# One encoder layer on one core: last short score tile of a head pair in a gate bank, one activation product behind the next difference, one operand's cast moved in its table

## The chip, the core and the metric

The kernel runs on one core of a Trainium2 chip. The core has a matmul engine (TensorE, in the profile PE, with its weight loads as PEld), a vector engine (VectorE, DVE), a scalar engine (ScalarE, ACT), a general engine (GpSimd, POOL) and a queue engine that issues most transfers (SyncE, SP). Matmul results go to PSUM banks and are read from there by DVE and ACT. The metric is the device time of one execution in microseconds (us); lower is better. Differences of less than about 0.2% of it, 4 us, can't be told from none.

## The reference, cut to what matters

One layer for two requests: a prompt of 1024 tokens and a sample of 32 tokens with caches, 1056 tokens in all, width 1024, feed-forward width 2816.

```python
h = _rms_norm(x, g_pre_mix)
z = h @ w_in
qa, ka, va, qb, fb, ib, ob, ga, gb = jnp.split(z, SPLIT_POINTS, axis=-1)
# A: sliding-window attention, 16 heads of width 64, 2 kv heads, sinks, relative bias
s = jnp.einsum('bnqkgd,bnskd->bnkgqs', q, k).astype(jnp.float32) * (A_HEAD_DIM ** -0.5)
...
p = jnp.exp(s - m)
denom = jnp.sum(p, axis=-1, keepdims=True) + jnp.exp(sink - m)
ya = jnp.einsum('bnkgqs,bnskd->bnqkgd', (p / denom).astype(v.dtype), v)
# B: gated linear recurrence, 8 heads
yb, s_fin = _hgrn2(...)
mix = jax.nn.sigmoid(ga) * (ya @ w_br_a) + jax.nn.sigmoid(gb) * (yb @ w_br_b)
x = x + _rms_norm(mix @ w_out, g_post_mix)
hf = _rms_norm(x, g_pre_ffn)
a, u = jnp.split(hf @ w_up, 2, axis=-1)
...                                   # ac: causal convolution of a over 3 tokens
ffn = (jax.nn.gelu(ac, approximate=True) * u) @ w_down
x = x + _rms_norm(ffn, g_post_ffn)
x = x + (pe @ w_ple) * jax.nn.sigmoid(x @ w_ple_gate)
```

## The kernel before

Everything is computed with activations transposed, features on the 128 partitions and tokens along the row. Each fp32 operand is split in two parts, a high one (a cast on ACT) and a low one (the difference, on DVE), and a product is three matmuls: high by high, high by low, low by high (`product`, L203 to L205). The engines run side by side, each through its own list of instructions in order; a scheduler makes those lists from the program, and where the code says `behind(engines)`, what is issued inside must stand behind the last instruction already issued on those engines. An instruction waits on semaphores for its inputs and for the last reader of a buffer that it is to write.

**Scores and gates.** Tokens lie in three groups of 384, 384 and 288. The heads are worked in eight pairs i. Around the scores of a pair run blocks of `w_in` columns (the next pair's q, and gates), each into a bank of the tag "mm". A pair has nine score tiles j: 0 to 7 for the prompt and 8 for the sample (64 rows, "short"). For a tile, `scores` makes the scores in a bank "s", softmax runs over them on DVE and ACT (probabilities `sc`, or `sc8` for tile 8; L509 to L514), `turn` transposes the probabilities into a bank (L535, for tile 8 L529) and splits them in a high and a low part (`split`: L226 on ACT, L227 on DVE), and `values` multiplies them by the values (L554, L555) into a bank "o" and adds the parts up (L561 on ACT, L562 and L563 on DVE). For tile 8 the result of `values` lies in the same bank as the turned probabilities, in its last quarter (`o8`), so that bank is held until L563 has read it. A q block that is done is split by `q_out`: L416 (ACT), L417 (DVE), L419 (ACT), L420 (DVE); a gate block is read by L295 (ACT). PSUM has here three banks "mm", two "tr", two "s" and one "o" (L238 to L248), each tag used in rotation. `turn` takes an "mm" bank for tiles 4 and 7, and a "tr" bank else. In four of the pairs (`H_AT`) DVE also adds up sums of h for a later stage (`h_sums`, L574 and on).

**The end of the second stage.** Before the up units, `ple_product` runs over four groups with a table `beside` of small steps between its matmuls: `at(m, f, ..., on=engines)` puts f at step m, behind what the named engines have been given. Among them are the last operands of the up units' products, made in place from four quarters b11, b21 (the page z[2]) and b12, b22 (z[3]): `minus` subtracts (L1899), L1919 adds, and `op_part(1, j, src)` casts a quarter to its high part (L1685, ACT) and takes the low part (L1686, DVE). The results of `ple_product` are copied out on ACT (L1732) and stored with a transfer that POOL issues (L1734).

**The up units.** For each of the 22 blocks of 128 features, `up_unit` makes both halves of the up product, for all tokens, by a scheme of seven products (0 to 6) over quarters of the operands, in three double banks X, Y, Z ("st"). The weights come split: L1756 (ACT), L1757 (DVE), with sums that POOL makes (L1770). After the products, `after(i)` takes what is ready: L2020 copies X to s1c (ACT), L2022 takes a difference U2, L2024 writes part of `ab`, L2027 writes nU3 = Y - s1c, L2029 and L2031 write the second half `us`, L2038 and others the rest. s1c, U2, nU3 and t12 lie in one tile `Sp`, the page that z[3] held. For product 5 PE writes Y again, so it must wait for L2027; for product 6 it writes Z again and waits for L2029. Unit 0 is run in two passes, over half of the tokens each; in the others a product is 24 matmuls of 264 columns (two halves of the tokens, four row blocks, the three lines L2009 to L2011).

`ff_tail(f, ab, u)`, a generator, is the rest of a unit: convolution (L1945, L1949, L1953), Gelu (L1954, ACT), the activation product (L1955 for 1024 columns, L1956 for the 32 of the sample) and its store act_d (L1957, on SP). Its first piece runs at the end of its unit (`done`), the rest behind product 1 of the next unit (`tail_rest`).

Of the kernel before, what the change touches and what calls it, by code (L numbers as in the profile page):

```python
# [21 lines left out]
NF = 22  # L22
# [37 lines left out]
def layer_kernel(  # L60
# [17 lines left out]
    def nm(s):  # L78
        n_names[0] += 1
        return f"{s}_{n_names[0]}"  # L80
# [5 lines left out]
    V, S, G, E = nc.vector, nc.scalar, nc.gpsimd, nc.tensor  # L86

    def behind(*engines):

        st = ExitStack()  # L90
        for e in engines:
            ins = next(i for i in reversed(nc.cur_bb.bb.instructions) if i.engine == e.engine)
            st.enter_context(tc.issue_after(ins))
        return st
# [128 lines left out]
    def split(hi, lo, src, scale=None):  # L223

        if scale is None:
            S.copy(hi, src)  # L226
            V.tensor_tensor(lo, src, hi.bitcast(F32), op=ALU.subtract)  # L227
        else:
            S.mul(hi, src, scale)
            V.scalar_tensor_tensor(lo, src, scale, hi.bitcast(F32), op0=ALU.mult, op1=ALU.subtract)  # L230

    def bank(pool, tag, bufs):
        return pool.tile([P, 512], F32, tag=tag, name=nm(tag), bufs=bufs)
# [4 lines left out]
    def mm_bank():  # L238
        return bank(pp, "mm", 3)

    def tr_bank():
        return bank(pp, "tr", 2)
# [35 lines left out]
    def unit(out):  # L278

        cell = []  # L280

        def get_w():
            if not cell:
                cell.append(next_w())
            return cell[0]
        return [(get_w, g, out) for g in range(3)]
# [4 lines left out]
    def gate_out(dst):  # L291
        def out(g, b):
            o, n = GR[g]
            t = gtile()
            S.activation(t[:, :n], b[:, :n], AF.Tanh, scale=0.5)  # L295
            dma(dst[:, o:o + n], t[:, :n])
        return out
# [17 lines left out]
    with right("ap") as ap:  # L315
# [148 lines left out]
        def span(j):  # L464

            if j == 8:
                return 32, 1024, 160, 0, ((8, 0, P), (9, P, 32))
            if j == 0:
                return P, 0, P, P, ((0, P, P),)
            return P, (j - 1) * P, 256, 0, ((j - 1, 0, P), (j, P, P))  # L470
# [48 lines left out]
        def turn(i, j):  # L519
            m_, k0, nk, b0, tl = span(j)  # L520
            sc = probs.get((i, j))
            ph = aq.tile([P, 2, 2 * P], F32R, tag="ph", name=nm("ph"), bufs=4)
            pl = aq.tile([P, 2, 2 * P], F32R, tag="pl", name=nm("pl"), bufs=4)
            t = mm_bank() if j in (4, 7) else tr_bank()
            n = 2 * len(tl) * m_
            ph, pl = (x[:].rearrange("p a b -> p (a b)")[:, :n] for x in (ph, pl))
            if j == 8:
                for a in range(2):
                    E.transpose(t[:, a * P:(a + 1) * P], sc8[:, a * P:(a + 1) * P], ident[:])  # L529
                split(*(x.rearrange("p (a b) -> p a b", b=64) for x in (ph, pl)),  # L530
                      t[:, 0:2 * P].rearrange("p (a b) -> p a b", b=P)[:, :, :64])
            else:
                for a, (_, kc, _) in enumerate(tl):
                    for h in range(2):
                        E.transpose(t[:, (2 * a + h) * P:(2 * a + h + 1) * P], sc[:, h, kc:kc + P],  # L535
                                    ident[:])
                split(ph, pl, t[:, :n])
            probs[i, j] = (ph, pl)
            if j == 8:
                o8[i] = t[:, 2 * P:3 * P]  # L540
# [387 lines left out]
        for i in range(8):  # L928
# [7 lines left out]
            if i == 0:  # L936
                rows_at = [lambda n=n: v_rows[n]() for n in range(9)] + [cache_parts]
                rows_at += [lambda n=n: k_rows[n]() for n in range(2)]
                for m, f in zip((0, 0, 1, *range(2, 20)), rows_at):
                    on = (E, S, V) if f is cache_parts else (E,)  # L940
# [17 lines left out]
            for j in range(9):  # L958
                at = lo_ + (hi_ - lo_) * j // 9
# [119 lines left out]
    with right("bp") as bp:  # L1079
# [311 lines left out]
        def at(m, f, *a):  # L1391
            small.setdefault(m, []).append(lambda: f(*a))
# [50 lines left out]
        u, v = (unit(gate_out(dst)) for dst, _ in GATES[14:])  # L1443
# [27 lines left out]
    with right("mp") as mp:  # L1471
# [33 lines left out]
        for b_, (c, g) in enumerate(order):  # L1505
            if c == len(ws):
                ws.append(next_w())
            o, n = G4[g]
# [311 lines left out]
    def prepare(n):  # L1820

        while n_parts[0] < min(n + 1, 7 * NF):
            u, i = divmod(n_parts[0], 7)
            if i == 0:
                if u not in raw_w:
                    unit_raw(u)
                s1 = wp.tile([P, 4, P], F32, tag="wb", name=nm("sa"), bufs=8)[:]
                gens[u] = unit_parts(u, s1, part_tile, lambda i, t: ready_w.append(t))
            next(gens[u])
            if i == 3 and u + 1 < NF:  # L1830
                unit_raw(u + 1)
            n_parts[0] += 1
# [40 lines left out]
    t = tr_bank()  # L1873
# [27 lines left out]
    def q_rows(g, i):  # L1901
        return z[g][:, 4 * i:4 * i + 4, :].bitcast(F32)

    b11, b21, b12, b22 = q_rows(2, 0), q_rows(2, 1), q_rows(3, 0), q_rows(3, 1)
# [13 lines left out]
    at(21, minus, b12, b22)  # L1918
    at(21, lambda: V.tensor_tensor(b22, b22, b11, op=ALU.add))  # L1919
    at(23, op_part, 1, 1, b22, on=(S,))  # L1920
    at(23, minus, b21, b22)
    at(25, op_part, 1, 3, b12, on=(S,))
    for g in range(4):
        ple_product(g, beside)
    assert not beside
# [9 lines left out]
    def ff_tail(f, ab, u):  # L1935

        w0, w1, w2 = (cvec[:, j * NF + f:j * NF + f + 1] for j in range(3))
        bc = cvec[:, 3 * NF + f:3 * NF + f + 1]
        n = T + 2
        a = fp.tile([P, T + 2], F32, tag="a", name=nm("a"), bufs=2)  # L1940
        V.tensor_copy(tails[:, 0, :, f], ab[:, 1024:1026])
        V.tensor_copy(tails[:, 1, :, f], ab[:, 1058:1060])
        with behind(V):
            V.tensor_copy(ab[:, 1026:1028], cach[:].rearrange("p (j f) -> p j f", j=2)[:, :, f])
        S.activation(a[:], ab[:, 0:n], AF.Identity, scale=w0, bias=bc)  # L1945
        if f < 3:
            V.tensor_tensor(u, u, rbT[:], op=ALU.mult)
            yield
        V.scalar_tensor_tensor(a[:], ab[:, 1:1 + n], w1, a[:], op0=ALU.mult, op1=ALU.add)  # L1949
        if f > 2:  # L1950
            V.tensor_tensor(u, u, rbT[:], op=ALU.mult)
            yield
        V.scalar_tensor_tensor(a[:], ab[:, 2:2 + n], w2, a[:], op0=ALU.mult, op1=ALU.add)  # L1953
        S.activation(a[:], a[:], AF.Gelu_apprx_tanh)  # L1954
        V.tensor_tensor(u[:, 0:1024], a[:, 0:1024], u[:, 0:1024], op=ALU.mult)  # L1955
        V.tensor_tensor(u[:, 1024:T], a[:, 1026:1058], u[:, 1024:T], op=ALU.mult)  # L1956
        dma(act_d[f][:], u)  # L1957
        yield

    tail_of = []  # L1960

    def tail_rest():
        for t in tail_of:
            next(t)
        tail_of.clear()

    def last_ops(n):

# [23 lines left out]
    def up_unit(u):  # L1992
# [7 lines left out]
        def mults(i, t, first, ps):  # L2000
            n = 7 * u + i
            if i not in w:
                w[i] = ready_w[n]
            for p in ps:
                for k in range(4):
                    wh, wl = w[i][:, 0, k, :], w[i][:, 1, k, :]
                    xh, xl = ops[p][i][:, 0, k, :], ops[p][i][:, 1, k, :]
                    o = t[:, p, 0:H]
                    E.matmul(o, wh, xh, start=first and k == 0, stop=False, skip_group_check=True)  # L2009
                    E.matmul(o, wh, xl, start=False, stop=False, skip_group_check=True)  # L2010
                    E.matmul(o, wl, xh, start=False, stop=k == 3, skip_group_check=True)  # L2011
# [43 lines left out]
        for ps, steps in (((0,), first_), ((1,), early)) if u == 0 else (((0, 1), order),):  # L2055
            for n, (i, t, first, then) in enumerate(steps):
                if u:
                    prepare(7 * u + n + AHEAD)
                elif ps == (1,):
                    with behind(S, V):  # L2060
                        prepare(n + AHEAD + 2)
                mults(i, t, first, ps)
                if ps == (1,) and n == 1:
                    with behind(E):
                        x1_t.append(pair_norm(1, 1.0 / D, late=True))
                if ps == (1,) and n == 4:
                    with behind(E):
                        x1_t[0]()
                for a in then:
                    with behind(*((V,) if ps == (0,) and a == 2 else ())):  # L2070
                        after(a, ps)
                if n == 1:
                    with behind(V):
                        tail_rest()
                if u == 0 and ps == (0,):
                    last_ops(n)
        done()
# [2 lines left out]
    for u in range(NF):  # L2080
        if u == 1:
            Up = page(lq, 2, [P, 2, T], "Up")
        if u == NF - 1:
            limit[0] = len(plan)
            load_raw()
            load_raw()
        up_unit(u)
    tail_rest()


    chunk_at = (("l4", "r3"), ("l6", "r5"), ("l7", "r6"), ("r0", "r7"))
# [103 lines left out]
    for s, dst in ((0, o_pconv), (1, o_sconv)):  # L2195
        b = tr_bank()
        E.transpose(b[:44, 0:P], tails[:, s].rearrange("p j f -> p (j f)"), ident[:])
        t = ep.tile([44, P], F32, tag="t", name=nm("tl"), bufs=6)
# [97 lines left out]
```

## Time and profile before

| | |
|---|---|
| median of three runs | 1984.14 us (1982.86 to 1984.45) |
| the profiled execution | 1983.89 us |
| its span | 1982.1 us |
| granted clock of TensorE | 0.999 |
| instructions | 37207 |
| turns of the score tiles (L535), in the span | 65.3 to 341.0 us |
| up units, first L2020 to last L1956 | 1167.5 to 1631.6 us |

The profile is of one execution. Times in it count from the start of its span, and the time of the execution is the span and 1.8 us around it. A row of the timeline gives start, duration, engine, line, operation, what is written and what is read with their shapes; in brackets stands how long the engine had been idle before it, and which instruction of another engine released it by the profile's reckoning. That name is the one that came last by the semaphores, and can be a neighbour of the true one. Rows of the view of waits have engine, line, whom it waited for, and then us in all, times and the longest.

### The profile page before, as it was taken

How to read it: one execution, taken by the hardware profiler on the slowest of the kernel's cores; microseconds unless marked ns; L12 is line 12 of the kernel's file. 1: busy time of each engine (PE TensorE's matmuls, PEld its weight loads, DVE VectorE, ACT ScalarE, POOL GpSimd, SP SyncE). 2: the span in 40 equal slices, each digit the busy share in tenths (PEclk: the TensorE clock that was granted, in tenths of full speed). 3: DMA queues.
4: the chain of work that ended last, by engine and by line, in shares of the span. 5: the costliest groups of instructions: out<-in, count | busy, mean ns of one | idle time of the engine just before them, and what ended most of it. 6: DMA issues, size and time to landing. Idle time of an engine off the chain costs nothing.

```text
span 1982.1 us, 37207 instructions
## 1 busy us (share of the span) xinstructions
PE 1962.2 (99%) x14239; PEld 1947.3 (98%) x14239; DVE 1387.5 (70%) x3059; ACT 1003.5 (51%) x2188; POOL 258.2 (13%) x391
## 2 busy tenths in 40 slices
PE   8999999999999999999999999999999999999998
PEld 8999999999999999999999999999999999999998
DVE  6777776888888888653555878877777784655552
ACT  7667767666656666451225663333333344444332
POOL 2111110000000000012001133333343300000000
PEclk9999999999999999999999999999999999999999
DMA  8533432311122121486558672222222255665542
GB/s 268 156 90 104 129 111 59 129 47 58 56 79 58 55 59 54 127 254 214 181 164 277 207 235 87 76 87 65 89 74 77 86 164 187 213 196 171 163 135 78
DMA packets 255256, 253.57 MB, mean 128 GB/s; under 512 B 14133, under 2 KB 221992, under 8 KB 255077
## 3 DMA queue, kind: packets, MB, share of 16 engines
q1 hardware_dynamic: 244917, 218.43, 35.3%
q0 software_dynamic: 10080, 32.73, 5.4%
q8 instruction: 112, 1.84, 0.4%
q14 instruction: 67, 0.55, 0.1%
q10 hardware_dynamic: 80, 0.03, 0.0%
HBM read 177.89 MB, written 65.32 MB: 123 GB/s over the span
## 4 chain that ended last, share of the span: by engine, by line
PE 90%; DVE 4%; ACT 2%; issue 2%; DMA 1%; POOL 0%; SPq 0%; DVEq 0%; ACTq 0%; POOLq 0%
PE mm L203 13%; PE mm L205 13%; PE mm L204 13%; PE st L2011 7%; PE st L2010 7%; PE st L2009 7%; PE G L1114 2%; PE Y L1111 2%; PE G L1113 2%; PE Y L1114 2%; PE G L1111 2%; PE Y L1113 2%; PE Z L1111 1%; PE Z L1113 1%; PE Z L1114 1%
## 5 line engine op out<-in xcount | busy, mean ns | idle before, releaser
L2009 PE MATMUL st<-op,wt 128*128 128x264 f32 x1232 | 348.7, 283 | 3.2 <-DVE Sp L2027 2.1
L2011 PE MATMUL st<-op,wt 128*128 128x264 f32 x1232 | 349.8, 284 | 0.0
L2010 PE MATMUL st<-op,wt 128*128 128x264 f32 x1232 | 347.7, 282 | 0.0
L2009 PEld LDWEIGHTS st<-op,wt 128*128 128x128 f32 x1232 | 231.2, 188 | 4.6 <-DVE Sp L2027 2.5
L2010 PEld LDWEIGHTS st<-op,wt 128*128 128x128 f32 x1232 | 231.4, 188 | 0.0
L2011 PEld LDWEIGHTS st<-op,wt 128*128 128x128 f32 x1232 | 230.9, 187 | 0.0
L182 ACT CAST wh<-wr 128x1024 fp32r<-128x1024 f32 x125 | 131.2, 1050 | 188.4 <-PE mm L204 146.2
L184 DVE TENSOR_TENSOR wl<-wr,wh 128x1024 fp32r<-128x1024 f32 x114 | 139.5, 1224 | 111.7 <-ACT wh L182 99.7
L1756 ACT CAST wt<-wu 128x512 fp32r<-128x512 f32 x126 | 77.8, 619 | 185.8 <-POOL ab L1995 82.3
L203 PE MATMUL mm<-ac,wh 128*128 128x352 f32 x528 | 170.6, 323 | 0.0
L205 PE MATMUL mm<-ac,wl 128*128 128x352 f32 x528 | 169.7, 321 | 0.0
L204 PE MATMUL mm<-ac,wh 128*128 128x352 f32 x528 | 169.4, 321 | 0.0
L203 PE MATMUL mm<-La,wh 128*128 128x384 f32 (+1 forms) x480 | 158.2, 330 | 0.0
L204 PE MATMUL mm<-Lb,wh 128*128 128x384 f32 (+1 forms) x480 | 155.3, 324 | 0.6 <-DVE Lb L773 0.6
L205 PE MATMUL mm<-La,wl 128*128 128x384 f32 (+1 forms) x480 | 154.8, 323 | 0.2 <-DVE wl L748 0.2
L203 PE MATMUL mm<-Ra,wh 128*128 128x264 f32 x512 | 145.4, 284 | 0.0
L204 PE MATMUL mm<-Rb,wh 128*128 128x264 f32 x512 | 145.0, 283 | 0.0
L205 PE MATMUL mm<-Ra,wl 128*128 128x264 f32 x512 | 145.0, 283 | 0.0
L1757 DVE TENSOR_TENSOR wt<-wu,wt 128x512 fp32r<-128x512 f32 x126 | 100.9, 803 | 47.1 <-ACT wt L1756 47.0
L205 PEld LDWEIGHTS mm<-ac,wl 128*128 128x128 f32 x528 | 99.4, 188 | 0.0
L204 PEld LDWEIGHTS mm<-ac,wh 128*128 128x128 f32 x528 | 99.3, 188 | 0.0
L203 PEld LDWEIGHTS mm<-ac,wh 128*128 128x128 f32 x528 | 99.0, 188 | 0.0
(553 smaller groups left out, 5746.4 us busy)
## 6 DMA issues: line engine op xcount, KB each, us to landing
wr<-in_w_down_dram SPq DMA_DIRECT2D x66, 512.0 KB
wu<-in_w_up_dram SPq DMA_DIRECT2D x42, 512.0 KB
wu<-in_w_in_dram SPq DMA_DIRECT2D x36, 512.0 KB
ac<-act_d SPq DMA_DIRECT2D x66, 176.0 KB
act_d<-Up SPq DMA_DIRECT2D x21, 528.0 KB
wr<-in_w_in_dram SPq DMA_DIRECT2D x21, 512.0 KB
wr<-in_w_out_dram SPq DMA_DIRECT2D x16, 512.0 KB
wl<-wr POOLq DMA_DIRECT2D x11, 512.0 KB, 4.9
```

Of the source, the lines that this page charges most:

```text
L182: S.copy(hi[:], raw[:])
L184: V.tensor_tensor(lo[:], raw[:], hi[:].bitcast(F32), op=ALU.subtract)
L203: E.matmul(ps, wh, a, start=first and n == 0, stop=False)
L204: E.matmul(ps, wh, b, start=False, stop=False)
L205: E.matmul(ps, wl, a, start=False, stop=last and n == len(ks) - 1)
L1111: E.matmul(o, wh, x[0][k], start=first and k == 0, stop=False, skip_group_check=True)
L1113: E.matmul(o, wh, x[1][k], start=False, stop=False, skip_group_check=True)
L1114: E.matmul(o, wl, x[0][k], start=False, stop=k == 3, skip_group_check=True)
L1757: V.tensor_tensor(t[:, 1], src, t[:, 0].bitcast(F32), op=ALU.subtract)
L2009: E.matmul(o, wh, xh, start=first and k == 0, stop=False, skip_group_check=True)
L2010: E.matmul(o, wh, xl, start=False, stop=False, skip_group_check=True)
L2011: E.matmul(o, wl, xh, start=False, stop=k == 3, skip_group_check=True)
```

## The change

There are three parts. `turn` takes an "mm" bank for tile 8 too, so that its values result lies in that bank as well. In `ff_tail` the unit 0 tail gets one more stop between Gelu and the activation product: `tail_rest(u)` no longer clears the list in unit 1, and behind product 3 of unit 1, after its `after(3)`, it is called again and runs the product and its store. (For f of 1 and more there is no such stop.) In the table `beside`, the step that casts operand 3 of the second half is put at 23, and the subtraction b21 - b22 at 25; they change places.

```diff
-            t = mm_bank() if j in (4, 7) else tr_bank()
+            t = mm_bank() if j in (4, 7, 8) else tr_bank()
...
     at(23, op_part, 1, 1, b22, on=(S,))
-    at(23, minus, b21, b22)
-    at(25, op_part, 1, 3, b12, on=(S,))
+    at(23, op_part, 1, 3, b12, on=(S,))
+    at(25, minus, b21, b22)
...
         S.activation(a[:], a[:], AF.Gelu_apprx_tanh)
+        if f < 1:
+            yield
         V.tensor_tensor(u[:, 0:1024], a[:, 0:1024], u[:, 0:1024], op=ALU.mult)
         V.tensor_tensor(u[:, 1024:T], a[:, 1026:1058], u[:, 1024:T], op=ALU.mult)
         dma(act_d[f][:], u)
...
-    def tail_rest():
+    def tail_rest(u):
         for t in tail_of:
             next(t)
-        tail_of.clear()
+        if u != 1:
+            tail_of.clear()
...
                 if n == 1:
                     with behind(V):
-                        tail_rest()
+                        tail_rest(u)
+                if u == 1 and n == 3:
+                    with behind(V):
+                        tail_rest(0)
...
-    tail_rest()
+    tail_rest(NF)
```

Behind `ff_tail` the lines of the changed kernel stand two or three higher: L1955 is L1957 there, L1956 is L1958, L2020 is L2023, L2022 is L2025, L2024 is L2027, L2027 is L2030, L2029 is L2032.

On PE, at tile 8 of a pair, the rows were these (the second s and the mm are the next score tile and the next block; what an instruction waits for stands in brackets, as engines):

```order
L529 MATMUL tr_2068<-ident,sc_811 128x128 [waits DVE_49,PE_49,Activation_49]
L529 MATMUL tr_2068<-ident,sc_811 128x128 [waits Pool_49]
L498 MATMUL s_2075<-K_0_186,qa_1627 128x256 [waits PE_49]
L499 MATMUL s_2075<-K_0_188,qa_1627 128x256
L498 MATMUL s_2075<-K_0_186,qb_1628 128x256
L499 MATMUL s_2075<-K_0_188,qb_1628 128x256
L203 MATMUL mm_2090<-La_177,wh_1576 128x384 [waits Activation_49]
L204 MATMUL mm_2090<-Lb_181,wh_1576 128x384
```

and they are now:

```order
L529 MATMUL mm_2068<-ident,sc_811 128x128 [waits DVE_49,Activation_49]
L529 MATMUL mm_2068<-ident,sc_811 128x128 [waits Pool_49]
L498 MATMUL s_2075<-K_0_186,qa_1627 128x256 [waits PE_49]
L499 MATMUL s_2075<-K_0_188,qa_1627 128x256
L498 MATMUL s_2075<-K_0_186,qb_1628 128x256
L499 MATMUL s_2075<-K_0_188,qb_1628 128x256
L203 MATMUL mm_2090<-La_177,wh_1576 128x384 [waits DVE_49]
L204 MATMUL mm_2090<-Lb_181,wh_1576 128x384
```

No row changes its place; tile 8 has another bank, and the block behind it waits for DVE and no longer for ACT.

On DVE, in up unit 1 (us is unit 0's second half, wt the split weights, Sp holds nU3), the rows were these:

```order
L2024 TENSOR_TENSOR ab_15178<-st_15175,rbT 128x2x264
L1757 TENSOR_TENSOR wt_15352<-wu_15130,wt_15352 128x512
L1955 TENSOR_TENSOR us_14887<-a_15168,us_14887 128x1024
L1956 TENSOR_TENSOR us_14887<-a_15168,us_14887 128x32
L2027 TENSOR_TENSOR Sp_14888<-st_15176,Sp_14888 128x528
L1757 TENSOR_TENSOR wt_15395<-wu_15132,wt_15395 128x512
L2029 TENSOR_TENSOR Up_15174<-Sp_14888,st_15177 128x2x264
```

and they are now:

```order
L2027 TENSOR_TENSOR ab_15178<-st_15175,rbT 128x2x264
L1757 TENSOR_TENSOR wt_15352<-wu_15130,wt_15352 128x512
L2030 TENSOR_TENSOR Sp_14888<-st_15176,Sp_14888 128x528
L1957 TENSOR_TENSOR us_14887<-a_15168,us_14887 128x1024
L1958 TENSOR_TENSOR us_14887<-a_15168,us_14887 128x32
L1757 TENSOR_TENSOR wt_15395<-wu_15132,wt_15395 128x512
L2032 TENSOR_TENSOR Up_15174<-Sp_14888,st_15177 128x2x264
```

The difference stands ahead of the two parts of the product; what comes behind is as it was.

On ACT, at the end of `ple_product` (op_14835 is operand 3 before, op_14819 in the changed kernel, op_14816 operand 1 in both; Sp is s1c of unit 0), the rows were these:

```order
L1732 COPY ple_14779<-st_14801 128x528
L1732 COPY ple_14820<-st_14821 128x528
L1685 CAST op_14835<-z_13343 128x1056
L1732 COPY ple_14820<-st_14838 128x528
L1732 COPY ple_14853<-st_14854 128x528
L1685 CAST op_14816<-z_13343 128x1056
L1732 COPY ple_14853<-st_14868 128x528
L2020 COPY Sp_14888<-st_14889 128x264
```

and they are now:

```order
L1732 COPY ple_14779<-st_14801 128x528
L1732 COPY ple_14822<-st_14823 128x528
L1732 COPY ple_14822<-st_14838 128x528
L1732 COPY ple_14853<-st_14854 128x528
L1685 CAST op_14816<-z_13343 128x1056
L1685 CAST op_14819<-z_13343 128x1056
L1732 COPY ple_14853<-st_14868 128x528
L2023 COPY Sp_14888<-st_14889 128x264
```

The cast of operand 3 stood two copies ahead of operand 1's, and now stands right behind it. On DVE the low parts (L1686) of the two follow in the same order: operand 3's, which stood ahead of the last L1899, is now the last of all.

## The prediction

> **What bounds the kernel now.** I read the busy line of the page first, then the chain of waits, then the list of what each engine waited for, and then the timeline around each place that the change touches.
>
> ```profile
> PE 1962.2 (99%) x14239; PEld 1947.3 (98%) x14239; DVE 1387.5 (70%) x3059; ACT 1003.5 (51%) x2188; POOL 258.2 (13%) x391
> PE 90%; DVE 4%; ACT 2%; issue 2%; DMA 1%; POOL 0%; SPq 0%; DVEq 0%; ACTq 0%; POOLq 0%
> PE tr L535 <- ACT qb L419: 3.4, 5, 0.8
> PE st L2009 <- DVE Sp L2027: 2.1, 2, 1.9
> PE st L2009 <- ACT Sp L2020: 0.9, 1, 0.9
> ```
>
> TensorE (PE) is busy for 1962.2 of 1982.1 us, and neither its matmuls nor their sizes change. So the change can only be worth what it adds to or takes from PE's stops. The three last rows (engine, line, whom it waited for: us in all, times, longest) are the three stops near the three edits: 6.4 us together, and a ceiling for what is to be gained, but for the small correction that follows. A matmul starts about 0.12 us after the one before it though each runs 0.28 (1206.50 and 1206.62 below), so a stop costs about 0.16 more than its idle figure.
>
> **First edit: the bank of the last short score tile.** The stop stands at the turn of a new head pair:
>
> ```profile
> 151.23 0.50 ACT L514 ACTIVATE sc<-sc,st 128x256 f32<-128x256 f32 x1
> 151.57 0.55 DVE L417 SCALAR_TENSOR_TENSOR qa<-mm,qa 64x384 fp32r<-64x384 f32 x1
> 151.84 0.29 PE L205 MATMUL mm<-La,wl 128*128 128x288 f32 x1
> 152.16 0.48 ACT L419 ACTIVATE qb<-mm 64x384 fp32r<-64x384 f32 x1
> 152.35 0.19 DVE L563 TENSOR_TENSOR ya<-tr,u 64x32 f32<-64x32 f32 x1
> 152.69 0.63 PE L535 MATMUL tr<-ident,sc 128*128 128x128 f32 x4 [0.56 <-ACT qb L419]
> 153.23 0.56 DVE L420 SCALAR_TENSOR_TENSOR qb<-mm,qb 64x384 fp32r<-64x384 f32 x1
> ```
>
> The view names L419, but a transpose of probabilities has no use for qb, and L419 ends at 152.64, just beside another candidate: the last read of the tr bank that tile 8 and its values sit in, L563, which ends at 152.54, 0.15 before PE starts again. There are two tr banks; the turn at 152.69 is the second one after tile 8, so it needs tile 8's bank. L563 is late because it stands on VectorE (DVE) behind L417. With tile 8 in an mm bank this turn needs only a tr bank that was read long before and its probabilities, ready at 151.73 (L514); PE comes at about 151.97. The stop goes. Over five boundaries that is 3.4 + 5 x 0.16 = 4.2 us, the most this edit can bring.
>
> What it adds is waits on the mm banks, three in rotation. The block of matmuls after tile 8 now takes the bank of turn 7, and tile 8 takes the one that the gate block left:
>
> ```profile
> 138.77 0.47 ACT L295 ACTIVATE gt<-mm 128x384 f32<-128x384 f32 x1
> 142.23 0.69 DVE L227 TENSOR_TENSOR pl<-mm,ph 128x512 fp32r<-128x512 f32 x1
> 143.46 0.38 PE L529 MATMUL tr<-ident,sc 128*128 128x128 f32 x2
> 144.16 0.34 PE L203 MATMUL mm<-La,wh 128*128 128x384 f32 x1
> ```
>
> Tile 8 at 143.46 needs L295, over at 139.24: 4.2 us early. The block at 144.16 needs turn 7's low part, over at 142.92: 1.24 us early. Both cost nothing, but if that low part were 1.24 us later, PE would stop there, with the four score matmuls and the whole block behind it.
>
> Where does the removed time go next? PE comes earlier to turns whose banks DVE or ScalarE (ACT) empty at a pace of their own:
>
> ```profile
> 161.94 0.41 ACT L295 ACTIVATE gt<-mm 128x288 f32<-128x288 f32 x1
> 163.04 0.60 PE L535 MATMUL mm<-ident,sc 128*128 128x128 f32 x4
> 223.79 0.63 PE L535 MATMUL tr<-ident,sc 128*128 128x128 f32 x4 [0.84 <-ACT qb L419]
> 224.86 0.56 DVE L574 TENSOR_TENSOR hs<-La,Lb 128x384 f32<-128x384 f32 x1
> 225.45 0.42 DVE L227 TENSOR_TENSOR pl<-tr,ph 128x256 fp32r<-128x256 f32 x1
> 226.34 0.60 PE L535 MATMUL tr<-ident,sc 128*128 128x128 f32 x4
> 176.00:211.00 35.00, 34.29 (x244) 34.02 (x242) 23.14 (x77) 25.99 (x69) 3.93 (x14) 1.00 0.45 124
> 211.00:247.00 36.00, 35.16 (x248) 34.82 (x247) 27.35 (x86) 25.66 (x69) 6.83 (x19) 1.00 0.37 102
> ```
>
> At the third boundary (223.79, stop 0.84 + 0.16 = 1.0) DVE works without a pause through two sums of h (L574), so L227 still ends at 225.87, and the turn at 226.34 has only 0.47 to spare: about 0.32 of the 1.0 stays won, after the 0.15 of a restart. The fourth boundary reads the same, 35.6 us later. At the first (0.72) the turn at 163.04 has 0.69 to spare on L295 (over at 162.35): about 0.6 stays. In the second and fifth there are no sums of h (the windows, in order us, PE, PEld, DVE: 23.14 us of DVE against 27.35), so they keep all, 4.2 - 0.72 - 1.0 - 0.73 = 1.75. Together 0.6 + 0.32 + 0.32 + 1.75 = **-3.0 us**, between -1.8 (if the second and fifth keep only a third, 0.6) and -4.2. The last head's turns are put in a new order on PE; the stops in it are a few tenths each, and I take **-0.2**, between +0.3 and -0.4, as an estimate.
>
> **Second edit: the first unit's activation product behind the difference.** In up unit 1:
>
> ```profile
> 1203.09 1.22 DVE L1955 TENSOR_TENSOR us<-a,us 128x1024 f32<-128x1024 f32 x1
> 1203.29 2.14 POOL L1770 TENSOR_TENSOR wu<-wu 128x512 f32<-128x512 f32 x1 [1.14 <-DVE wt L1757]
> 1204.23 1.26 DVE L1956 TENSOR_TENSOR us<-a,us 128x32 f32<-128x32 f32 x1
> 1205.41 0.69 DVE L2027 TENSOR_TENSOR Sp<-st,Sp 128x528 f32<-128x528 f32 x1
> 1206.16 0.39 PE L2009 MATMUL st<-op,wt 128*128 128x264 f32 x1 [1.87 <-DVE Sp L2027]
> 1206.50 0.28 PE L2011 MATMUL st<-op,wt 128*128 128x264 f32 x1
> 1206.62 0.28 PE L2009 MATMUL st<-op,wt 128*128 128x264 f32 x1
> 1206.62 0.69 DVE L2029 TENSOR_TENSOR Up<-Sp,st 128x528 f32<-128x528 f32 x1
> L1770 POOL TENSOR_TENSOR wu<-wu x21: 1287/1295/2171, 1187.4 to 1591.5; 128x512 f32<-128x512 f32 x21
> ```
>
> PE would have come to its next product at 1206.16 - 1.87 - 0.16 = 1204.13. L2027 now takes L1955's place, 1203.09 to 1203.78, so the stop of 2.03 goes. The two products then come next, and L2029, after the same five instructions as before, still ends at 1207.31. The last of the seven products of the unit needs it, and PE comes there 24 x 0.12 = 2.9 after 1204.13, at 1207.0, where before it came two us later and found it done. That is a new stop of about 0.3. The store of the activation leaves up to 0.7 us later on SP's queue; it is read back only when the last product of the layer begins, and hides behind the other units. Net **-1.8**, between -1.4 and -2.03.
>
> L1956 takes 1.26 for 32 columns and ends with the GpSimd sum L1770 (1205.43), which itself takes 2.14 here against a median of 1.295: the two hold each other up. The Trainium skill ("SBUF — State Buffer", section "Who interferes with whom") has the rule: a DVE instruction with two SBUF inputs and a GpSimd instruction that reads SBUF exclude each other for their whole length, first come first served; the trace agrees. By that rule L1770 would now come first, since L2027 has one input in PSUM, and run to about 1204.6; the products would end near 1206.0 and the new stop shrink to 0.2, a net of -1.9 where my row sum has -1.8.
>
> **Third edit: the last operand's cast.** Its words say sooner. The rows of the order say otherwise: the cast of operand 3 stood on ACT ahead of two copies, one of which waits on a transfer, and now stands behind them and behind operand 1's cast.
>
> ```profile
> 1161.14 1.09 ACT L1685 CAST op<-z 128x1056 fp32r<-128x1056 f32 x1
> 1164.57 0.60 ACT L1732 COPY ple<-st 128x528 f32<-128x528 f32 x1 [1.84 <-DMA ple_d<-ple]
> 1166.18 1.26 DVE L1686 TENSOR_TENSOR op<-z,op 128x1056 fp32r<-128x1056 f32 x1 [0.99 <-ACT op L1685]
> 1167.52 0.38 ACT L2020 COPY Sp<-st 128x264 f32<-128x264 f32 x1 [0.88 <-DVE op L1686]
> 1167.96 0.39 PE L2009 MATMUL st<-op,wt 128*128 128x264 f32 x1 [0.87 <-ACT Sp L2020]
> 1176.58 2.43 DVE L1686 TENSOR_TENSOR op<-z,op 128x1056 fp32r<-128x1056 f32 x2
> ```
>
> Before, operand 3 was cast at 1161.14 and split on DVE long before the end; the last L1686 is operand 1's, 1166.18 to 1167.44. L2020 writes a page that held the source rows of both operands, so it waits for the last of them, and PE waits 0.87 for L2020. Now a second split of L1686 follows: two in a row take 2.43, one takes 1.26, so 1.17 more, and PE's third product of unit 0 stands until about 1169.1. Cost **+1.1** (a tenth may be absorbed at a later stop of that unit), between 0 and +1.3. The wait on the transfer at 1164.57 cannot cover it, since both casts now stand behind it.
>
> **The sum**: -3.0 - 0.2 - 1.8 + 1.1 = -3.9 us. The profiled execution took 1983.89 with a span of 1982.1, and would take 1980.0; the median of the runs shown is 1984.14, 0.25 above it, so **1980.2**.
>
> **Rivals.** (B) The removed stop only moves: DVE, at 23 to 27 of 35 us, holds PE again at a later turn in all five boundaries, and edit 1 brings 1.5 rather than 3.2. For it: the 0.47 at 226.34. Against: two heads without sums of h. Sum -1.5 - 1.8 + 1.1 = -2.2, 1981.9. (C) The cast costs nothing, since L2020 turns out to wait for other readers than operand 3's split, or the landing at 1164.57 comes earlier: -5.0, 1979.1. Against it: L2020 started 0.08 after the last split. (D) The change does not do what it says, because the turn really waits for L419, which the view names: then 4.2 us of stops stay, and -1.8 + 1.1 = -0.7 gives 1983.4. (E) Slower: the mm rotation, now with tile 8 in it, gives the block at 144.16 a bank that a q block has just filled, and so waits for its drain through L416, L417, L419 and L420. In the boundary shown that drain ends at 153.79, and the stretch from L417's start is 2.2 us; seven heads at about 2.2 make +15, less 3.9, so 1995. It decides from the point where the block's first matmul waits for L420 and not for L227. The order shows that matmul waiting on DVE alone, where L227 is the last reader of turn 7, so I give it little.
>
> **How the numbers follow.** The forecast 0.60, B 0.14, C 0.14, D 0.04, E 0.08. A change under 0.2% (4.0 us, so 1980.17) cannot be told from none in a measurement of this kernel. The forecast lies almost on that line: of its 0.60 I put 0.33 below it, 0.27 above. Faster 0.33 + 0.14 = 0.47; same 0.27 + 0.14 + 0.04 = 0.45; slower 0.08. The forecast's own ends: -1.8 + 0.3 - 1.4 + 1.3 is -1.6, and -4.2 - 0.4 - 2.0 + 0 is -6.6; the ends will not meet, so I keep 1977.9 to 1982.3 for it. The range reaches over B and D to 1983.4 and leaves out E.
>
> **What would show it.** Right: the L535 row of waits on L419 falls from 3.4 to under 1, with new short waits on L227 and L295 at the third, fourth and first boundaries; the L2027 row falls under 0.3, and an L2029 row of about 0.3 appears; the L2020 row grows from 0.9 to about 2. Wrong: L535 still stopping beside L419 (D), an L203 stop on L420 or L227 of more than 1 us per head (E), or the L2020 row unchanged (C).

## The result, and the profile after

In 20 runs of each kernel the median went from 1985.28 to 1981.42 us, 3.9 less; the ratio is 0.9982 with a 95% interval of 0.9975 to 0.9988, which is 2.4 to 5.0 us. The interval leaves out zero, so the kernel is faster. The 0.18% is just under the 0.2% that was set as the line, and by that line it counts as no change. The profiled execution has a span of 1980.2 us, only 1.9 under that of before; where the other two went is shown below.

The page of the changed kernel, its busy line, and its view of waits for PE at the three places (engine, line, whom it waited for: us in all, times, longest):

```profile
PE 1963.0 (99%) x14239; PEld 1948.0 (98%) x14239; DVE 1388.1 (70%) x3059; ACT 1003.0 (51%) x2188; POOL 259.2 (13%) x391
```

```profile
PE st L2012 <- ACT Sp L2023: 1.4, 2, 0.9
PE tr L535 <- DVE pl L227: 0.9, 3, 0.5
...
PE st L2012 <- ACT ple L1732: 0.7, 1, 0.7
...
PE st L2012 <- DVE us L2032: 0.3, 1, 0.3
...
PE st L2012 <- DVE Sp L2030: 0.2, 1, 0.2
```

PE is as busy as before. The row of L535 on L419 (3.4) is gone, and one on L227 (0.9) is in its place: 0.47 and 0.20 at two pair boundaries, and 0.25 in the last pair. The row on the difference (2.1 on L2027) is down to 0.2 (L2030 now). The row on s1c has grown from 0.9 to 1.4, now in two stops, and there is a new one of 0.7 on a copy of L1732. The row of 0.3 on L2032 is one stop in unit 0, at 1173.39; the kernel before stops there for 0.2.

Since PE runs the same matmuls in nearly the same order, the two executions can be laid side by side matmul by matmul. The table has the time between four marks of PE's list: the first matmul, the first L535, the first matmul of the recurrence behind the scores (L1111), the first up product; then the next 168 matmuls of the list and the next 336. Matmuls of other steps stand among them (13 in the first 168, 11 in the next 336), so each of the last two columns ends a little before its unit does. The table is worked out from the starts in each trace, in us. The rest is nearly alike in all: 806.8 between scores and up units, 20.35 for unit 3, and 731.9 to 732.6 from there to the end (732.3 in both the kernel before and the changed one).

| kernel | start-up | scores | unit 0 | units 1 and 2 |
|---|---|---|---|---|
| before | 62.88 | 291.64 | 22.00 | 43.66 |
| the change | 64.11 | 288.50 | 23.12 | 42.41 |
| bank alone | 62.95 | 288.44 | 21.89 | 43.64 |
| product alone | 64.22 | 291.68 | 21.93 | 42.37 |
| cast alone | 63.55 | 291.68 | 24.87 (clock 0.50 for 3.4 us) | 43.67 |
| bank and product | 64.09 | 288.50 | 21.61 | 42.39 |
| and operand 1's cast ahead | 64.48 | 288.47 | 21.32 | 42.37 |
| bank, product, copy on ACT | 63.03 | 288.43 | 22.14 | 41.57 |
| bank, sums later | 63.72 | 287.61 | 22.09 | 45.20 (clock 0.50 for 3.4 us) |
| all of it | 63.57 | 287.61 | 21.70 | 41.58 |

The change: -3.14 in the scores, +1.12 in unit 0, -1.25 in units 1 and 2, together -3.27. The start-up is 1.23 longer, which makes -2.04, the difference of the two spans. That start-up belongs to the execution and not to the edits: it goes from 62.9 to 64.5 over these kernels, with 64.22 in one that leaves the scores as they were and 62.95 in one that changes them, and up to the first L535 PE, DVE, ACT and POOL run the same lists of instructions in all ten. So the profile of before was one of a short start, and the medians, -3.9 us, are nearer to the sum of the stages.

In two of the ten traces TensorE's granted clock falls to 0.50 for 3.4 us: from 1170.4 in the cast alone and from 1204.5 with the sums later. The matmuls start 0.22 apart there instead of 0.12, and about 1.5 us is lost each time. Both falls begin right behind 3.4 us in which PE had stood idle for 1.7 and 1.9 us: the first behind the two stops that the cast's move makes, the second behind the stop of 1.9 for the difference, which the kernel before has too. The traces of the kernel before and of the bank alone have that stop of 1.9 without such a fall. So a stop may cost more in some executions than its idle time says. That is one candidate for the 0.6 us by which the medians exceed the columns. Two traces show neither that the stop is the cause nor how often it happens, and the interval of the medians is wide enough for the 0.6 to be chance.

**The pair boundary.** The timeline of the changed kernel at the first one:

```profile
152.43 0.50 ACT L514 ACTIVATE sc<-sc,st 128x256 f32<-128x256 f32 x1
152.77 0.55 DVE L417 SCALAR_TENSOR_TENSOR qa<-mm,qa 64x384 fp32r<-64x384 f32 x1
153.17 0.60 PE L535 MATMUL tr<-ident,sc 128*128 128x128 f32 x4
153.36 0.49 ACT L419 ACTIVATE qb<-mm 64x384 fp32r<-64x384 f32 x1
153.55 0.19 DVE L563 TENSOR_TENSOR ya<-mm,u 64x32 f32<-64x32 f32 x1
```

The turn starts at 153.17 without any idle time, before L419 has even begun and before L563 has read tile 8's bank. It did not need qb; it needed the bank. At the third boundary the rows that give a part back:

```profile
222.56 0.60 PE L535 MATMUL tr<-ident,sc 128*128 128x128 f32 x4
224.62 0.56 DVE L574 TENSOR_TENSOR hs<-La,Lb 128x384 f32<-128x384 f32 x1
225.21 0.42 DVE L227 TENSOR_TENSOR pl<-tr,ph 128x256 fp32r<-128x256 f32 x1
225.69 0.66 PE L535 MATMUL tr<-ident,sc 128*128 128x128 f32 x4 [0.47 <-DVE pl L227]
```

The stop there is gone at 222.56, and most of it is back at 225.69, behind L227, which came at DVE's own pace. At the first boundary a smaller part comes back at the turn behind the gate block:

```profile
163.15 0.41 ACT L295 ACTIVATE gt<-mm 128x288 f32<-128x288 f32 x1
163.61 0.66 PE L535 MATMUL mm<-ident,sc 128*128 128x128 f32 x4
```

L295 ends at 163.56, 0.05 before the turn; before the change it had 0.69 to spare. No idle time is on record here, but PE loses 0.2 over this turn and the few matmuls behind it. The table has PE's lead over the kernel before, in us: what is won at the turn of the boundary, what comes back before the next one, and what is kept.

| boundary | won | given back | kept |
|---|---|---|---|
| first | 0.75 | 0.20 | 0.55 |
| second | 0.89 | 0 | 0.89 |
| third | 1.03 | 0.67 | 0.36 |
| fourth | 0.77 | 0.43 | 0.34 |
| fifth | 0.88 | 0.05 | 0.83 |

Together that is 2.97; the last pair brings 0.14 more, and 0.03 lies before the first boundary.

**The product in up unit 1.** DVE and GpSimd of the changed kernel:

```profile
1202.32 0.70 DVE L2030 TENSOR_TENSOR Sp<-st,Sp 128x528 f32<-128x528 f32 x1
1202.93 1.98 DVE L1957 TENSOR_TENSOR us<-a,us 128x1024 f32<-128x1024 f32 x1
1204.84 0.18 DVE L1958 TENSOR_TENSOR us<-a,us 128x32 f32<-128x32 f32 x1
1205.54 0.69 DVE L2032 TENSOR_TENSOR Up<-Sp,st 128x528 f32<-128x528 f32 x1
...
1202.54 1.29 POOL L1770 TENSOR_TENSOR wu<-wu 128x512 f32<-128x512 f32 x1 [1.14 <-DVE wt L1757]
```

Now GpSimd's sum is first and takes its median of 1.29. L1957 stands 0.9 behind it until 1203.83 and takes 1.98 instead of 1.22, and L1958 takes 0.18 instead of 1.26: from the start of the one to the end of the other it is 2.09 now, and was 2.40. L2032 is over at 1206.23, and PE comes to product 6 at 1206.29. It has no idle time there and loses 0.1. It stops in the next unit:

```profile
1212.49 1.28 DVE L1941 COPY tails<-ab 128x2 f32<-128x2 f32 x1
1213.69 0.16 DVE L1942 COPY tails<-ab 128x2 f32<-128x2 f32 x1
1213.76 0.16 DVE L1944 COPY ab<-cach 128x2 f32<-128x2 f32 x1
1213.95 1.27 ACT L1945 ACTIVATE a<-ab,cvec 128x1058 f32<-128x1058 f32 x1 [3.82 <-DVE ab L1944]
1215.13 0.57 ACT L2023 COPY Sp<-st 128x528 f32<-128x528 f32 x1
1215.76 0.39 PE L2012 MATMUL st<-op,wt 128*128 128x264 f32 x1 [0.48 <-ACT Sp L2023]
...
1212.47 1.28 POOL L1763 TENSOR_TENSOR sa<-wu 128x512 f32<-128x512 f32 x1 [8.63 <-PE st L2014]
```

A copy of two columns, 0.16 us before, takes 1.28: as long as L1763, which started 0.02 ahead of it. Behind it on DVE stands the small copy L1944, for that waits the convolution on ACT, behind that on ACT stands the copy of s1c, and for that waits PE. The same two in the timeline of the kernel before:

```profile
1214.30 0.16 DVE L1941 COPY tails<-ab 128x2 f32<-128x2 f32 x1
...
1215.23 1.28 POOL L1763 TENSOR_TENSOR sa<-wu 128x512 f32<-128x512 f32 x1 [9.80 <-PE st L2011]
```

There they did not meet. PE brought L1763 forward by 2.8, DVE's copies came only 1.8 earlier. The stop costs PE 0.7, in two steps: 0.64 at the matmul shown and 0.11 at the one behind it.

**The cast.** ACT and PE of the changed kernel in unit 0:

```profile
1162.66 0.60 ACT L1732 COPY ple<-st 128x528 f32<-128x528 f32 x1 [2.81 <-DMA ple_d<-ple]
1163.15 2.05 ACT L1685 CAST op<-z 128x1056 fp32r<-128x1056 f32 x2
1165.10 0.60 ACT L1732 COPY ple<-st 128x528 f32<-128x528 f32 x1
1166.78 0.38 ACT L2023 COPY Sp<-st 128x264 f32<-128x264 f32 x1 [1.07 <-DVE op L1686]
...
1165.76 0.39 PE L2012 MATMUL st<-op,wt 128*128 128x264 f32 x1 [0.73 <-ACT ple L1732]
1167.21 0.39 PE L2012 MATMUL st<-op,wt 128*128 128x264 f32 x1 [0.94 <-ACT Sp L2023]
```

Both casts now stand behind the copy that waits for a transfer, and ACT is idle for 2.81 ahead of it where it was 1.84. The last copy of the group stands behind both of them, and frees a bank that PE wants after the first two products of unit 0 (24 matmuls): 0.73 idle there, and two matmuls on the old stop of 0.9 again. What sets the time of the restart at 1167.21 is the copy of s1c, L2023, over at 1167.16. It starts 4.83 behind PE's first up product, against 3.65 in the kernel before: 1.18 later, the length of the second split of L1686. The stop on L1732 lies within that time and adds nothing to it.

### The profile page after: what moved, and what is told of

It is laid out like the page before. It is cut to its first block, busy times and chain, and to the rows that moved or that the text cites. A ratio compares the mean times of both kernels' runs of the same rounds, so it can differ in the third digit from the quotient of the medians.

```text
span 1980.2 us, 37208 instructions
## 1 busy us (share of the span) xinstructions
PE 1963.0 (99%) x14239; PEld 1948.0 (98%) x14239; DVE 1388.1 (70%) x3059; ACT 1003.0 (51%) x2188; POOL 259.2 (13%) x391
## 3 DMA queue, kind: packets, MB, share of 16 engines
q8 instruction: 112, 1.84, 0.4%
## 4 chain that ended last, share of the span: by engine, by line
PE 76%; issue 12%; DVE 5%; DMA 3%; ACT 2%; POOL 1%; SPq 0%; POOLq 0%; DVEq 0%; ACTq 0%
PE mm L203 9%; PE mm L205 9%; PE mm L204 9%; PE st L2014 7%; PE st L2012 7%; PE st L2013 7%; PE G L1114 2%; PE Y L1111 2%; PE G L1113 2%; PE Y L1114 2%; PE Y L1113 2%; PE G L1111 2%; PE Z L1111 1%; PE Z L1113 1%; PE Z L1114 1%
## 5 line engine op out<-in xcount | busy, mean ns | idle before, releaser
L203 PE MATMUL mm<-ac,wh 128*128 128x352 f32 x528 | 170.6, 323 | 0.0
L203 PE MATMUL mm<-La,wh 128*128 128x384 f32 (+1 forms) x480 | 158.2, 330 | 0.0
L203 PE MATMUL mm<-Ra,wh 128*128 128x264 f32 x512 | 145.4, 284 | 0.0
L203 PEld LDWEIGHTS mm<-ac,wh 128*128 128x128 f32 x528 | 99.1, 188 | 0.0
```

What stands on the lines that cost most here:

```text
L203: E.matmul(ps, wh, a, start=first and n == 0, stop=False)
```

## The experiments

All were timed against the kernel before, in the same sessions: 1985.36 us is its median for the first four, 1985.66 for the others.

**Bank alone.**

```diff
-            t = mm_bank() if j in (4, 7) else tr_bank()
+            t = mm_bank() if j in (4, 7, 8) else tr_bank()
```

> Only the bank of tile 8 is changed. Theory: PE's stops at the five pair boundaries go but for what is given back at the third and fourth, so PE is 3.0 to 3.1 us ahead of the kernel before at the end of the score stage and stays so: time -3.0 (ratio 0.9985). Rival (the stops only move, B): -1.5. Rival (the turn waited for L419, D): 0. If the later start-up seen in the profile after belongs to this edit, PE is again about 1.3 us late before the first pair; if it is chance, it is anywhere within some tenths to one us either way.

Median 1981.86, ratio 0.9984 (0.9975 to 0.9994). The scores take 288.44, 3.2 less than before, with the boundaries as in the table to 0.1 us, and the start-up 62.95. The theory holds; 0 and -1.5 are out by the stage, and the start-up is not the edit's.

**Product alone.**

```diff
         S.activation(a[:], a[:], AF.Gelu_apprx_tanh)
+        if f < 1:
+            yield
...
+                if u == 1 and n == 3:
+                    with behind(V):
+                        tail_rest(0)
```

> Only the activation product of unit 0 is moved behind the difference of unit 1. Theory: the stop of 2.0 in unit 1 goes, GpSimd's sum takes 1.3 and holds the product up (about 2.0 instead of 1.2 for 1024 columns, 0.2 for the 32), no new stop at L2032 in unit 1; GpSimd's next sums come some 2.8 us earlier and meet the 128x2 copy L1941, which takes 1.3, and a stop of 0.6 follows in unit 2. Net -1.4 (ratio 0.9993). Rival: without that meeting (the copy takes 0.16) there is no stop in unit 2, net -2.0.

Median 1983.55, ratio 0.999 (0.9981 to 0.9999). Units 1 and 2 take 42.37, 1.29 less: -2.12 at product 5 of unit 1, +0.08 at product 6, +0.75 in unit 2. The rival of no meeting is out. L1770 took 1.29, L1957 1.98, L1958 0.18, and L1941 1.28, as in the whole change.

**Cast alone.**

```diff
-    at(23, minus, b21, b22)
-    at(25, op_part, 1, 3, b12, on=(S,))
+    at(23, op_part, 1, 3, b12, on=(S,))
+    at(25, minus, b21, b22)
```

> Only the two table entries change places. Theory: the last low part of the operands ends 1.17 us later, and PE loses 1.1 us more in unit 0: time +1.1 (ratio 1.0006). Rival (C, the cast costs nothing): 0 or below. Rival: the second copy of the last group, now behind two casts, is what PE waits for: then a stop beside L1732 of 0.7 or more is there, and the loss beside L2023 stays at 0.9.

Median 1986.02, ratio 1.0005 (0.9997 to 1.0014): the time alone does not tell it from nothing. The trace does: PE stops 0.7 for L1732 and 0.9 for L2020, as in the whole change, and the steps there against the kernel before are +0.89, -0.95, +1.00 and +0.10. A stop for L2029, 48 matmuls further on, grows by 0.13, which makes +1.17. (The fall of TensorE's clock just behind makes the stage longer still in this execution.) The price is the one forecast, and the rival of no cost (C) is out. The second of the two rivals is right about where PE stops, but what sets the restart is the path of the theory, the last low part and s1c's copy.

**Bank and product, without the cast.**

> Bank and product without the table's change. Theory: the edits add up, -3.0 and -1.4 make -4.4 (ratio 0.9978), about 1.1 faster than the whole change. Rival (C): the same as the whole change, -3.4 to -3.9.

Median 1979.86, ratio 0.9972 (0.9961 to 0.9982), 1.6 under the whole change by the medians, whose intervals overlap. The scores and units 1 and 2 are -3.14 and -1.27 against the kernel before, and unit 0 is at 21.61, where the kernels with the same table have 21.9 to 22.1: in this execution the copy behind the transfer waited for 1.46 only, not 1.84, which gives about 0.4 that is not the edit's. Rival (C) is out by the stage, 23.12 against these, and not by the medians.

**Operand 1's cast ahead of the waiting copy**, on top of bank and product:

```diff
-    at(23, op_part, 1, 1, b22, on=(S,))
     at(23, minus, b21, b22)
     at(25, op_part, 1, 3, b12, on=(S,))
+    at(28, op_part, 1, 1, b22, on=(S,))
...
-                S.copy(t[:, c % 4 - 1:c % 4 + 1, :], b[:, :, :H])
+                with behind(*((S,) if (g, c) == (3, 5) else ())):
+                    S.copy(t[:, c % 4 - 1:c % 4 + 1, :], b[:, :, :H])
```

> Bank and product, and operand 1's cast (b22) pinned ahead of the copy on ACT that waits for a transfer. Theory: what holds PE in unit 0 is the cast that stands behind that wait; the last low part then ends about 1.1 us earlier, the stop of 0.9 to 1.0 beside s1c's copy goes, and the kernel is 1.0 faster than bank and product alone (1979.9 there, so 1978.9; about -5.5 by the steps of the profile). Rival: the stop stays since something else holds the copy: 0.

Median 1978.98, ratio 0.9968 (0.9956 to 0.9980), 0.9 under bank and product. ACT of this kernel, and then DVE:

```profile
1161.33 1.08 ACT L1685 CAST op<-z 128x1056 fp32r<-128x1056 f32 x1 [0.16 <-DVE z L1920]
1162.76 1.10 ACT L1733 COPY ple<-st 128x528 f32<-128x528 f32 x2 [0.34 <-DMA ple_d<-ple]
1164.89 0.38 ACT L2024 COPY Sp<-st 128x264 f32<-128x264 f32 x1 [1.03 <-DVE op L1686]
...
1163.56 1.25 DVE L1686 TENSOR_TENSOR op<-z,op 128x1056 fp32r<-128x1056 f32 x1
```

The cast runs in the time that ACT stood idle, the last low part follows the subtraction before it without a gap, and PE has no stop at s1c's copy in unit 0. Of the 1.06 won there some 0.7 stays (unit 0 at 21.32 against 22.0 in the kernel before; 0.3 against the 21.61 of bank and product, with its short wait for the transfer); 0.4 comes back at a stop later in the unit, on L2026. The 0.9 of the medians is below what these runs resolve. This is what the words of the change wanted, an operand's cast sooner: but it is the other operand's.

**The small copy on ACT**, on top of bank and product:

```diff
-        with behind(V):
-            V.tensor_copy(ab[:, 1026:1028], cach[:].rearrange("p (j f) -> p j f", j=2)[:, :, f])
+        S.copy(ab[:, 1026:1028], cach[:].rearrange("p (j f) -> p j f", j=2)[:, :, f])
```

> Bank and product, and the 128x2 copy from the cache into ab taken off DVE and given to ACT, so that the convolution on ACT no longer stands behind DVE's 128x2 copies. Theory: the stop of 0.6 in unit 2 comes from the copy L1941, held up by GpSimd's sum; with the convolution free of it the stop goes, though L1941 itself may still take 1.3. 0.6 faster than bank and product alone. Rival: PE's earlier arrival is the cause, and 0.5 to 0.6 of a stop stays at the same place.

Median 1979.60, ratio 0.9968 (0.9957 to 0.9980). Units 1 and 2 take 41.57 against 42.39, 0.8 less. DVE, GpSimd and ACT of this kernel in unit 2:

```profile
1210.17 0.16 DVE L1941 COPY tails<-ab 128x2 f32<-128x2 f32 x1
1210.29 1.22 DVE L1942 COPY tails<-ab 128x2 f32<-128x2 f32 x1
...
1210.18 1.30 POOL L1763 TENSOR_TENSOR sa<-wu 128x512 f32<-128x512 f32 x1 [8.66 <-PE st L2013]
...
1210.29 1.27 ACT L1944 ACTIVATE a<-ab,cvec 128x1058 f32<-128x1058 f32 x1 [2.44 <-DVE ab L2047]
```

The meeting is still there: L1941, 0.01 ahead of GpSimd's sum, takes its 0.16, and this time the second copy is held until GpSimd is done. Nobody waits for it now, and PE does not stop in unit 2. So the stop came from the held copy and not from PE's earlier arrival.

**Sums of h later**, on top of the bank:

```diff
-                    small.setdefault(lo_ + 2 * m + 1, []).append(
+                    small.setdefault(lo_ + 2 * m + 5, []).append(
```

> Bank alone, and the sums of h put four steps later in their pairs. Theory: the 0.59 and 0.33 given back at the third and fourth boundaries come from those sums on DVE; with them elsewhere all five stops go in full, 0.9 faster than bank alone (1981.0). Rival: DVE is as busy anyway, the same or other turns give it back: 0, or slower where the sums now meet something else.

The scores take 287.61 against 288.44, 0.83 less, and PE's row of L535 on L227 falls from 0.9 to 0.2, so the sums are what gave the two parts back: nothing comes back at the third and fourth boundaries. At the first 0.4 comes back instead of 0.1, at a turn that now waits for L420. The median, 1982.16 with a ratio of 0.998 (0.9971 to 0.9988), does not tell this from the bank alone, and lies 0.3 above its 1981.86 where 0.9 less was forecast; a difference of 0.8 is below what these runs resolve.

**All together.**

> Bank, product, operand 1's cast ahead, the copy on ACT and the sums later, together. Theory: they add up: -3.1 - 0.9 - 2.0 - 1.0 = -7.0, ratio 0.9965. Rival: where one of the three additions fails in its own run, by as much less.

Median 1978.03, ratio 0.9961 (0.9949 to 0.9973), which is 5.4 to 10.1 us under the kernel before, and 3.4 under the change by the medians. Scores 287.61, unit 0 21.70, units 1 and 2 41.58: against before -4.03, -0.30 and -2.08, in all -6.4 where -7.0 was forecast. Of the three additions the cast ahead brought least here, since stops of 0.3 and 0.4 came in unit 0 at other places. This is the fastest kernel of the study.

## Why the prediction was right, and where it was not

**The bound** was right: PE, and only its stops count. Three stops, three edits, and from the scores to the up units, and from unit 3 to the end, the rest of the program unmoved to 0.1 us. Only the start-up differs, with the same lists.

**Bank**: -3.2 forecast with the last pair, -3.14 measured. The releaser that the view names, L419, was the wrong one, as argued from the 0.15 between L563 and the restart. The turn now starts before L419 does. The sum holds term by term too: 0.55 is kept at the first boundary, on L295, where 0.6 was forecast; 0.36 and 0.34 at the third and fourth, behind L227, for 0.32 each; 0.89 and 0.83 at the second and fifth for 1.75 together; and 0.14 comes in the last pair for 0.2. (The fourth boundary stands 35.3 us behind the third, and not 35.6; nothing hangs on it.) The rivals are out: no effect (D) and a mere move (B) by the -3.14, a q block's drain (E) since no L203 stop on L227 or L420 appears in the list.

**Product**: -1.8 forecast (its own terms, -2.03 and +0.3, make -1.7), -1.25 measured. The stop itself went as forecast. The term that failed is the last one: "That is a new stop of about 0.3", in unit 1 at L2029. There PE loses 0.1, since the two products were shorter together; instead 0.7 came in unit 2, at a copy that the prediction does not name. The row of 0.3 on L2032 looks like the sign that was set for it, but that stop is in unit 0.

The rule of the Trainium skill ("SBUF — State Buffer", section "Who interferes with whom") had this pair right, and the trace agrees: L1770 comes first and takes its plain 1.29, the products stand behind it, the new stop is smaller. The prediction took the rule to be worth 0.1 us and followed it to one pair of instructions only.

Moving GpSimd's sums by 2.8 us was enough to bring two others together, L1763 and the copy L1941 of the next unit's tail. L1941 reads only one SBUF tile, so the rule in the prediction's words does not cover it; here the trace alone shows the hold: 1.28 us instead of 0.16, over at 1213.77, and L1763 over at 1213.75.

**Cast**: +1.1 forecast, +1.12 measured in the change and +1.17 alone. That it goes later and not sooner was read from the order. The path was right as well: a second split, then s1c's copy 1.18 later, then PE. What was missed is where PE stands in that time. The prediction put all of it on L2023, a row of about 2; but L1732 of the same group is behind both casts too, PE stops there for 0.7 on the way, and the L2023 stop of unit 0 kept its 0.9. (The row of 1.4 has 0.5 from unit 2 in it.)

**The sum**: -3.9 forecast, -3.9 by the medians of 20 runs, -3.27 by the stages. That the first two agree to a tenth is luck: the interval of the medians is 2.4 to 5.0, and by the stages the forecast was 0.6 too much, nearly all of it in the product. The time itself came out 1.2 above the 1980.2 forecast, since the three runs of before that I had gave a median 1.1 under that of twenty. The chances of faster and of no change were nearly alike, and the result, 0.18%, lies almost on the line between them.

## What to carry to other kernels

A releaser in a view of waits is the last to come, not always the one needed: ask what the waiting instruction can have use for, and which buffer it writes. An edit that frees one engine moves the others against each other, so follow the second one (here GpSimd) to the next place where it meets a neighbour. A list of idle times does not show every loss: 0.2 at the first boundary and 0.1 at product 6 are seen only when two traces are laid side by side. An order table says where a step is asked for; where it lands is read from each engine's list, and a step that is put behind a wait for a transfer is late by that wait, whatever its number.

## What the runs showed of the hardware that I had not expected

A DVE copy of 128x2, 0.16 us by itself, took 1.28 us when a GpSimd sum of 128x512 had started 0.02 us earlier. With the small copy on ACT, the first copy started 0.01 ahead of the sum and took 0.16, and its neighbour, 0.11 behind it, took 1.22.

TensorE's clock fell to half for 3.4 us in two of ten traces, each time behind a stretch in which PE had been idle for half of the time, and 1.5 us was lost; the cause is not shown.

The start-up, with the same lists on four engines, varied from 62.9 to 64.5 us between executions, 1.6 us where the change is worth 3.9. Between the scores and the up units the ten traces agree to 0.1 us, and behind unit 3 to 0.7, where medians of many runs have intervals of 2 us and more.
